# 64 bytes of padding behind the split-weight and transposed-x buffers of a two-layer decoder trunk

## The chip, the cores and the metric

The kernel runs on one core of one Trainium2 chip. The metric is the device time of the whole program in microseconds (us); lower is better. The kernel before was timed in three runs: 1771.68, 1772.74 and 1776.7 us, median 1772.74 us.

## The reference

The program computes a two-layer causal decoder trunk on x of 256 tokens by 2048 channels in float32. Cut to what matters for the time:

```
for layer in (0, 1):
    x = x + mixer(rmsnorm(x))          # layer 0: conv module and sparse attention, with w_in (2048 x 4656), w_out (2048 x 2048)
                                       # layer 1: pooling mixer, four 512 x 512 maps
    h = rmsnorm(x) @ w1                # w1: 2048 x 8192
    x = x + square(relu(h)) @ w2       # w2: 8192 x 2048
return rmsnorm(x)
```

## The kernel before, in words

Every large matrix product is done in three passes, to keep float32 precision with a one-pass matmul format: a weight w is split into a rounded part `hi` and a rest `lo`, an activation X likewise into Xh and Xl, and the product is hi*Xh + hi*Xl + lo*Xh. Each such triple is three matmuls on TensorE, each with a stationary operand of 128x128 that is loaded first (a row PEld in the profile) and a moving operand of 256 or 512 columns that streams through.

The weights are used in some 390 units of 128 partitions x 2048 floats (8192 bytes in a partition). The class `Weights` loads a unit into one of three `wraw` buffers by DMA from SyncE's queue, then splits it in two or four pieces: ScalarE writes `whi` (line 147) and VectorE subtracts to get `wlo` (recorded at line 78, where a small wrapper calls VectorE). `whi` and `wlo` have three buffers each, used in turn. Transposed x lies in four `xT` buffers of 8192 bytes, one for each group of 512 channels; each holds four k-tiles, with 256 columns of Xh and 256 of Xl in each.

The order of all instructions is written out by the program: no scheduler reorders it. Two kinds of matmul groups alternate.

- **256-column matmuls**: `unit_cols` (mixer) and `unit_wide` / `first_hidden` (MLP) load a 128x128 piece of `whi` or `wlo` as stationary operand and stream 256 columns of `xT`. One unit of weights meets the four `xT` buffers one after the other, 12 matmuls for each.
- **512-column matmuls**: `product` and its like load a 128x128 piece of the split hidden activations (buffers f11, f12, s1 to s4 and f22, shown in rows as `f` or `s`) and stream 512 columns of `whi` or `wlo`. `by_token` does the same in the output projection, with stationary pieces of `yo` (which lies in two `xT` buffers) or of `yc`.

An MLP layer runs over eight chunks of hidden channels. Inside the loop over seven of them each chunk does 8 tiles of 48 matmuls with 256 columns (the next chunk's hidden values) and 14 products of 12 matmuls with 512 columns (a Strassen-like scheme; VectorE adds weight units in `z` and `b` for it). So the two layers have 14 such chunks.

All matmuls are recorded at line 194 (a wrapper `mm`); transposes at line 232. So groups of rows are told apart by their tiles' names.

Of the kernel before, what the change touches and what calls it, by code (L numbers as in the profile page):

```python
# [27 lines left out]
F32 = mybir.dt.float32  # L28
F32R = mybir.dt.float32r
# [5 lines left out]
P = 128  # L35
S = 256
D = 2048
# [13 lines left out]
WARM = 2  # L51
RHO, SLACK, CATCH_UP = 0.99, 1.0, 1.1
W_BUFS = 3

CHUNKS = 8
MIX_UNITS = 52
# [26 lines left out]
class Weights:  # L83
# [13 lines left out]
    def load(self, pieces=1):  # L97
        u, n = self.loaded, D // pieces
        use = self.uses[u]
        self.loaded += 1  # L100
        if "z" in use:
            for tiles, name, bufs in ((self.z, "z", 2), (self.b, "b", 1)):
                t = tiles[use["set"]] = self.zpool.tile([P, D], F32, tag=name, bufs=bufs, name=name)
                self.nc.sync.dma_start(t, self.src[use[name]])
        if "raw" not in use:
            return
        t = self.pool.tile([P, D], F32, tag="raw", bufs=RAW_BUFS, name="wraw")
        self.raw[u] = t
        for i in range(pieces):
            self.nc.sync.dma_start(t[:, i * n:(i + 1) * n], self.src[use["raw"], :, i * n:(i + 1) * n])  # L110
            yield
# [22 lines left out]
    def pieces(self):  # L134

        nc = self.nc
        while self.split < self.n:
            if self.split >= PLAIN:
                use = self.uses[self.split]
                raw = self.raw.pop(self.split) if "raw" in use else {"z": self.z, "b": self.b}[use["from"]][use["set"]]  # L140
                hi = self.pool.tile([P, D], F32R, tag="whi", bufs=W_BUFS, name="whi")
                lo = self.pool.tile([P, D], F32R, tag="wlo", bufs=W_BUFS, name="wlo")
                self.parts[self.split] = (hi, lo)
                cut = self.cut
                for h in range(cut):
                    c = slice(h * (D // cut), (h + 1) * (D // cut))
                    nc.scalar.activation(hi[:, c], raw[:, c], AF.Copy)  # L147
                    self.done = (h + 0.5) / cut
                    yield
                    if self.queue:  # L150
                        self.queue.pop(0)()
                    self.vector.tensor_sub(lo[:, c], raw[:, c], hi[:, c].bitcast(F32))
                    self.done = (h + 1) / cut
                    if h < cut - 1:
                        yield
                self.then(use, raw)
            self.split += 1
            self.done = 0.0
            yield
# [20 lines left out]
def trunk(ctx: ExitStack, tc: tile.TileContext, a: dict, out: bass.AP, dump: dict | None = None):  # L180
# [5 lines left out]
    act = ctx.enter_context(tc.tile_pool(name="act", bufs=1, side="left"))  # L186
# [42 lines left out]
    def transpose(out, src):  # L229
        n = src.shape[0]  # L230
        pe[0] += 0.218
        nc.tensor.transpose(out, src, ident[0:n, 0:n])  # L232

    def split_evac(hi, lo, src):
        nc.scalar.activation(hi, src, AF.Copy)
        vector.tensor_sub(lo, src, hi.bitcast(F32))

    xT = [None] * 4

    x = None  # L240

    def turn_x(dc, g0, bank):

        xT[dc] = act.tile([P, 4, 512], F32R, tag="xT", bufs=4, name="xT")
        rest = []
        for h in range(2):
            t = bank().rearrange("p (f t) -> p f t", f=2)
            for f in range(2):
                d = (4 * dc + 2 * h + f) * P
                for tok in range(2):  # L250
                    transpose(t[:, f, tok * P:(tok + 1) * P], x[:, tok, d:d + P])
            for f in range(2):
                dt = 4 * dc + 2 * h + f
                o, g = xT[dc][:, 2 * h + f], vec[:, g0 + dt:g0 + dt + 1]
                nc.scalar.activation(o[:, 0:256], t[:, f], AF.Copy, scale=g)
                rest.append(lambda o=o, t=t[:, f], g=g: vector.scalar_tensor_tensor(
                    o[:, 256:512], t, g, o[:, 0:256].bitcast(F32), op0=ALU.mult, op1=ALU.subtract))
        for r in rest:
            r()
# [16 lines left out]
    with ExitStack() as mx:  # L276
        mix = mx.enter_context(tc.tile_pool(name="mix", bufs=1, side="right", reuse_waits="tile"))
# [44 lines left out]
        def start_steps():  # L322
            yield lambda: (token_sum(sq[0][:, 0], pss), vector.tensor_copy(r0, rms(pss, CONV / D)))
            yield lambda: (to_rows(r0, acc1(), rbc), split_x())

        def split_x():
            lo = []
            for j in range(4):
                xn = xraw[:, 4 * j:4 * j + 4]
                vector.tensor_tensor(xn, x32[j // 2][:, 4 * (j % 2):4 * (j % 2) + 4],  # L330
                                        rbc[:, None].to_broadcast([P, 4, 256]), op=ALU.mult)
                t = act.tile([P, 4, 512], F32R, tag="xT", bufs=4, name="xT")
                nc.scalar.activation(t[:, :, 0:256], xn, AF.Copy)
                lo.append(lambda t=t, xn=xn: vector.tensor_sub(t[:, :, 256:512], xn, t[:, :, 0:256].bitcast(F32)))
                if j:
                    lo.pop(0)()
                xT[j] = t
            lo.pop(0)()
            W.hold = False
# [108 lines left out]
        for i in range(2):  # L448
            t = mix.tile([P, KT, P], F32, tag="q8", bufs=2, name="w1")
# [5 lines left out]
        for i in range(2):  # L455
            t = mix.tile([P, 512], F32, tag="tt", bufs=3, name="wgl")[:, 0:384]
# [154 lines left out]
        def bank(tag, dt=F32):  # L611
            return ps.tile([P, 512], dt, tag=tag, bufs=2, name=tag)
# [40 lines left out]
        def transposed():  # L653
            for s in Tt:
                if callable(Tt[s]):
                    Tt[s] = Tt[s]()
# [194 lines left out]
        yo = []  # L851

        def o_transposed(m, b):
            if not yo:
                yo.extend(act.tile([P, 4, 512], F32R, tag="xT", bufs=4, name="yo") for _ in range(2))
            transposed()
            tp = bank("T")
            for d2 in range(2):
                dt = 4 * m + 2 * b + d2
                for tok in range(2):  # L860
                    transpose(tp[:, d2 * 256 + tok * P:d2 * 256 + (tok + 1) * P], o_tok[:, tok, dt * P:(dt + 1) * P])
            split_evac(yo[m][:, 2 * b:2 * b + 2, 0:256], yo[m][:, 2 * b:2 * b + 2, 256:512],
                       tp.rearrange("p (d t) -> p d t", d=2))
# [3 lines left out]
        for j in range(8):  # L867
            if j == 7:
                steps[2] = both(steps[2], one(o_transposed, 0, 0))
                steps[3] = both(steps[3], one(o_transposed, 0, 1))  # L870
# [35 lines left out]
        xt = [None] * 4  # L906

        def load_x(i, n, tag, bufs):
            t = (act if tag == "xT" else mix).tile([P, 2, n * 512], F32, tag=tag, bufs=bufs, name="xt",
                                                   padded_shape=[P, 2, 1024])  # L910
            nc.sync.dma_start(t, a["xn"][:, :, i * 512:(i + n) * 512])
            for q in range(n):
                xt[i + q] = t[:, :, q * 512:(q + 1) * 512]

        load_x(0, 2, "xT", 4)
        load_x(2, 1, "xT", 4)

        def o_half():
# [62 lines left out]
        for dc, u in O_ORDER:  # L981
            if u == 0:
                accs[dc] = [bank3() for _ in range(2)]

            def finish():
                for tok in range(2):
                    vector.tensor_add(x[:, tok, dc * 512:(dc + 1) * 512], xt[dc][:, tok], accs[dc][tok])
                turns.extend([lambda: None, lambda dc=dc: turn_x(dc, V_MLP0, bank3)])

            out_unit(accs[dc], yc[u], u, beside_conv, finish)  # L990
# [241 lines left out]
    def after0(dc):  # L1232
        add_squares(dc, ssq1)
        if dc == 0:
            pm_parts.extend(load_pm(i) for i in range(3))
            ps_row.extend(row(a["pool_scale"]))
        elif pm_parts:
            pm_parts.pop(0)()
        return [lambda: turn_x(dc, V_MIX1, bank3)]
# [33 lines left out]
    def pool_and_first():  # L1273


        units = first_hidden([lambda dc=dc: turn_x(dc, V_MLP1, bank3) for dc in (1, 2, 3)])
        next(units)
        pool_mean(2, z2)
        next(units)
        pool_mean(3, z3)  # L1280
        yield from units
# [146 lines left out]
```

## Time and profile before

| what | value |
|---|---|
| three runs | 1771.68, 1772.74, 1776.7 us (median 1772.74) |
| the profiled execution's own time | 1777.96 us |
| its span, first to last instruction | 1776.2 us |
| mean granted TensorE clock | 0.997 of full speed |
| TensorE busy | 1752.6 us of the span (99%), 11726 matmuls |
| VectorE busy | 1518.5 us (85%) |
| ScalarE busy | 1084.6 us (61%) |

The busy time of TensorE is the union of its matmuls. The matmuls overlap, so the mean time of one (277 to 284 ns for 256 columns) is more than the time from one start to the next; how long a matmul holds the engine is read from the starts of rows in the timeline.

### The profile page before, as it was taken

What the parts mean: (1) busy time and instruction counts of PE and PEld (TensorE: products, weight loads), DVE (VectorE), ACT (ScalarE), POOL (GpSimd) and SP (SyncE); (2) the same over time, 40 slices, a digit from 0 to 9 for tenths busy, and PEclk for the clock granted to TensorE, in tenths of its full rate; (3) what the DMA queues carried; (4) which work ended last, traced back from release to release, by engine and by line L of the source; (5) the groups of instructions that cost most, each with busy time, mean ns of one, the idle gap of its engine ahead of it and who ended that gap; (6) DMA issues with size and microseconds to landing.
All of it is one profiled execution on the core that took longest, in us unless ns stands there. A gap on an engine that the chain in (4) does not pass through costs nothing.

```text
span 1776.2 us, 28729 instructions
## 1 busy us (share of the span) xinstructions
PE 1752.6 (99%) x11726; PEld 1595.4 (90%) x11726; DVE 1518.5 (85%) x1888; ACT 1084.6 (61%) x1626; POOL 59.7 (3%) x80
## 2 busy tenths in 40 slices
PE   9999999999999999999999999999999999999997
PEld 7999998889898899999898989988989898989885
DVE  6998997766989898898989868798988989898984
ACT  4445666547666666666666655766666666666663
POOL 1000000000000000000000000000000000000000
PEclk9999999999999999999999999999999999999998
DMA  7654323546778787878777764687878787778772
GB/s 274 237 197 143 120 96 134 199 167 227 259 248 253 236 248 236 276 230 295 232 248 247 230 228 155 232 256 238 257 237 271 233 294 233 249 243 259 247 245 97
DMA packets 58052, 399.89 MB, mean 225 GB/s; under 512 B 6560, under 2 KB 6960, under 8 KB 10816
## 3 DMA queue, kind: packets, MB, share of 16 engines
q1 hardware_dynamic: 47760, 333.47, 48.9%
q0 software_dynamic: 8576, 61.43, 18.5%
q10 hardware_dynamic: 1584, 3.16, 0.5%
q8 instruction: 92, 1.51, 0.3%
q14 instruction: 40, 0.33, 0.0%
HBM read 395.93 MB, written 2.10 MB: 224 GB/s over the span
## 4 chain that ended last, share of the span: by engine, by line
PE 78%; DVE 18%; ACT 2%; issue 1%; DMA 1%; ACTq 0%; POOLq 0%; SPq 0%; DVEq 0%
PE acc L194 73%; DVE wlo L78 9%; DVE z L78 3%; DVE s L78 3%; PE S L194 2%; DVE x L78 2%; PE PV L194 1%; ACT whi L147 1%; PE T L232 1%; PE acc L232 1%; DVE f L78 0%; DMA xraw<-in_xT 0%; ACT t L1026 0%; DMA ident<-in_ident 0%; ACT t L1025 0%
## 5 line engine op out<-in xcount | busy, mean ns | idle before, releaser
L194 PE MATMUL acc<-xT,whi 128*128 128x256 f32 x4992 | 872.1, 279 | 0.0
L194 PEld LDWEIGHTS acc<-xT,whi 128*128 128x128 f32 x4992 | 764.8, 188 | 10.1
L78 DVE TENSOR_TENSOR wlo<-wraw,whi 128x1024 fp32r<-128x1024 f32 (+1 forms) x552 | 604.9, 1126 | 143.7 <-ACT whi L147 142.8
L194 PE MATMUL acc<-xT,wlo 128*128 128x256 f32 x2496 | 694.0, 278 | 0.0
L147 ACT ACTIVATE whi<-wraw 128x1024 fp32r<-128x1024 f32 (+1 forms) x552 | 515.2, 974 | 105.1 <-PE acc L194 86.5
L194 PEld LDWEIGHTS acc<-xT,wlo 128*128 128x128 f32 x2496 | 470.7, 189 | 0.0
L194 PE MATMUL acc<-whi,s 128*128 128x512 f32 x960 | 318.5, 393 | 2.8 <-DVE s L78 1.6
L78 DVE TENSOR_TENSOR wlo<-z,whi 128x1024 fp32r<-128x1024 f32 x224 | 267.1, 1219 | 47.9 <-ACT whi L147 47.1
L147 ACT ACTIVATE whi<-z 128x1024 fp32r<-128x1024 f32 x224 | 230.5, 1054 | 94.2 <-DVE z L78 73.3
L194 PE MATMUL acc<-whi,f 128*128 128x512 f32 x864 | 283.0, 392 | 0.0
L194 PEld LDWEIGHTS acc<-whi,s 128*128 128x128 f32 x960 | 179.3, 188 | 42.2 <-DVE s L78 7.5
L1025 ACT ACTIVATE t<-acc 128x256 f32<-128x256 f32 x128 | 48.8, 381 | 251.6 <-PE acc L194 250.8
L194 PE MATMUL acc<-wlo,s 128*128 128x512 f32 x480 | 190.8, 397 | 1.1
L194 PEld LDWEIGHTS acc<-whi,f 128*128 128x128 f32 x864 | 162.4, 188 | 32.2
L194 PE MATMUL acc<-wlo,f 128*128 128x512 f32 x432 | 169.4, 392 | 0.0
L78 DVE SCALAR_TENSOR_TENSOR x<-acc,r,x 128x512 f32<-128x512 f32 x156 | 116.4, 746 | 14.4 <-PE acc L194 14.2
L194 PEld LDWEIGHTS acc<-wlo,s 128*128 128x128 f32 x480 | 90.1, 188 | 28.2 <-DVE wlo L78 9.7
L78 DVE SCALAR_TENSOR_TENSOR ctile<-ctile,cw 128x256 f32<-128x256 f32 x240 | 101.5, 475 | 0.1
L194 PEld LDWEIGHTS acc<-wlo,f 128*128 128x128 f32 x432 | 81.1, 188 | 16.0
L1070 ACT ACTIVATE s<-s 128x512 fp32r<-128x512 f32 x56 | 35.4, 632 | 72.1 <-DVE s L78 72.1
L78 DVE TENSOR_TENSOR z<-z,wraw 128x1024 f32<-128x1024 f32 x56 | 65.9, 1219 | 0.0
L78 DVE TENSOR_TENSOR z<-z,b 128x1024 f32<-128x1024 f32 x56 | 65.9, 1219 | 0.0
(206 smaller groups left out, 1361.4 us busy)
## 6 DMA issues: line engine op xcount, KB each, us to landing
wraw<-in_ws SPq DMA_DIRECT2D x254, 1024.0 KB, 6.3
z<-in_ws SPq DMA_DIRECT2D x28, 1024.0 KB, 7.4
b<-in_ws SPq DMA_DIRECT2D x28, 1024.0 KB, 4.8
b<-in_ws POOLq DMA_DIRECT2D x28, 1024.0 KB, 8.8
z<-in_ws POOLq DMA_DIRECT2D x28, 1024.0 KB, 8.2
xraw<-in_xT SPq DMA_DIRECT2D x4, 512.0 KB, 7.5
wraw<-in_ws SPq DMA_DIRECT2D x8, 256.0 KB, 7.4
w<-in_cmp_w POOLq DMA_DIRECT2D x2, 1024.0 KB, 7.6
```

Of the source, the lines that this page charges most:

```text
L78: return fn(*args, **kw)
L147: nc.scalar.activation(hi[:, c], raw[:, c], AF.Copy)
L194: nc.tensor.matmul(out, w, x, **kw)
L232: nc.tensor.transpose(out, src, ident[0:n, 0:n])
L1025: nc.scalar.activation(out, acc, AF.Relu)
L1070: nc.scalar.activation(F[tag][:, :, 0:P], src(), AF.Copy)
```

## The change

Every `whi`, `wlo` and `xT` buffer (and `yo`, which shares xT's buffers) gets 16 floats, 64 bytes, behind its 8192. The tiles themselves are cut back to the same 2048 floats. One load of x in `load_x` no longer asks for a padded shape. The order of the instructions, their shapes and their waits are the same on all engines; only addresses differ.

```
+SKEW = 16
...
-                hi = self.pool.tile([P, D], F32R, tag="whi", bufs=W_BUFS, name="whi")
-                lo = self.pool.tile([P, D], F32R, tag="wlo", bufs=W_BUFS, name="wlo")
+                hi = self.pool.tile([P, D + SKEW], F32R, tag="whi", bufs=W_BUFS, name="whi")[:, 0:D]
+                lo = self.pool.tile([P, D + SKEW], F32R, tag="wlo", bufs=W_BUFS, name="wlo")[:, 0:D]
...
+    def skewed(name):
+        t = act.tile([P, D + SKEW], F32R, tag="xT", bufs=4, name=name)
+        return t[:, 0:D].rearrange("p (k t) -> p k t", k=4)
...
-        xT[dc] = act.tile([P, 4, 512], F32R, tag="xT", bufs=4, name="xT")
+        xT[dc] = skewed("xT")
...
-                t = act.tile([P, 4, 512], F32R, tag="xT", bufs=4, name="xT")
+                t = skewed("xT")
...
-                yo.extend(act.tile([P, 4, 512], F32R, tag="xT", bufs=4, name="yo") for _ in range(2))
+                yo.extend(skewed("yo") for _ in range(2))
...
-            t = (act if tag == "xT" else mix).tile([P, 2, n * 512], F32, tag=tag, bufs=bufs, name="xt",
-                                                   padded_shape=[P, 2, 1024])
+            t = (act if tag == "xT" else mix).tile([P, 2, n * 512], F32, tag=tag, bufs=bufs, name="xt")
```

Where the buffers start in each partition, in bytes, in the two built programs (in brackets the start modulo 512):

| buffers | before | after |
|---|---|---|
| whi, three | 48928, 57120, 65312 (all 288) | 48928, 57184, 65440 (288, 352, 416) |
| wlo, three | 73504, 81696, 89888 (all 288) | 73696, 81952, 90208 (480, 32, 96) |
| xT, four | 115424, 123616, 131808, 140000 (all 224) | 115808, 124064, 132320, 140576 (96, 160, 224, 288) |
| f11 to f22, seven | 193504 to 225248 (all 480) | the same |
| yc, two | 155232, 163424 (both 96) | the same |
| wraw, three | 24352, 32544, 40736 (all 288) | the same |
| z, two | 168928, 177120 (both 480) | the same |

Within a tile, the pieces that one matmul loads or streams start at multiples of 512 bytes. So the distance from the streaming piece to the piece that is loaded meanwhile, modulo 512, is the same for all matmuls of one pair of buffers. Here "distance" is the start of the stationary piece less the start of the moving piece, modulo 512:

| loaded while streaming | before | after (i = 0 to 2 the weight buffer, j = 0 to 3 the xT buffer) |
|---|---|---|
| whi while xT streams | 64 | 192 + 64(i - j): 0 to 320 |
| wlo while xT streams | 64 | 384 + 64(i - j): 192 to 448, and 0 |
| f or s while whi streams | 192 | 192, 128, 64 |
| f or s while wlo streams | 192 | 0, 448, 384 |
| yo while whi or wlo streams | 448 | varies |
| yc while whi streams | 320 | 320, 256, 192 |
| yc while wlo streams | 320 | 128, 64, 0 |

## Rows read from the trace of the kernel before

**Rows 1.** The page's head and its busy time of two engines.
```profile
span 1776.2 us, 28729 instructions
...
PE 1752.6 (99%) x11726; PEld 1595.4 (90%) x11726; DVE 1518.5 (85%) x1888; ACT 1084.6 (61%) x1626; POOL 59.7 (3%) x80
```

**Rows 2.** The page's chain that ended last, by engine and by line.
```profile
PE 78%; DVE 18%; ACT 2%; issue 1%; DMA 1%; ACTq 0%; POOLq 0%; SPq 0%; DVEq 0%
PE acc L194 73%; DVE wlo L78 9%; DVE z L78 3%; DVE s L78 3%; PE S L194 2%; DVE x L78 2%; PE PV L194 1%; ACT whi L147 1%; PE T L232 1%; PE acc L232 1%; DVE f L78 0%; DMA xraw<-in_xT 0%; ACT t L1026 0%; DMA ident<-in_ident 0%; ACT t L1025 0%
```

**Rows 3.** Costliest matmul groups, whole span: count | busy us, mean ns | idle before.
```profile
L194 PE MATMUL acc<-xT,whi 128*128 128x256 f32 x4992 | 872.1, 279 | 0.0
L194 PE MATMUL acc<-xT,wlo 128*128 128x256 f32 x2496 | 694.0, 278 | 0.0
L194 PE MATMUL acc<-whi,s 128*128 128x512 f32 x960 | 318.5, 393 | 2.8 <-DVE s L78 1.6
L194 PE MATMUL acc<-whi,f 128*128 128x512 f32 x864 | 283.0, 392 | 0.0
```

**Rows 4.** Timeline of PE, first and last row of one stretch: start, length.
```profile
748.27 0.28 PE L194 MATMUL acc<-xT,wlo 128*128 128x256 f32 x1
...
752.87 0.28 PE L194 MATMUL acc<-xT,wlo 128*128 128x256 f32 x1
```

**Rows 5.** The same for a later stretch, with its first row after 512-column matmuls.
```profile
798.07 0.40 PE L194 MATMUL acc<-xT,whi 128*128 128x256 f32 x2
...
799.00 0.28 PE L194 MATMUL acc<-xT,wlo 128*128 128x256 f32 x1
...
803.42 0.28 PE L194 MATMUL acc<-xT,wlo 128*128 128x256 f32 x1
```

**Rows 6.** The chain in order of time: start, length, what; five chunks' pieces.
```profile
534.05 58.60 PE acc L194 x394
618.51 58.60 PE acc L194 x394
702.98 58.60 PE acc L194 x394
787.45 57.36 PE acc L194 x394
870.67 57.36 PE acc L194 x394
```

**Rows 7.** One matmul group in the windows 37:270, 537:786 and 1125:1715 us.
```profile
L194 PE MATMUL acc<-xT,wlo 128*128 128x256 f32 x444 | 124.6, 281 | 0.0
...
L194 PE MATMUL acc<-xT,wlo 128*128 128x256 f32 x383 | 107.7, 281 | 0.0
...
L194 PE MATMUL acc<-xT,wlo 128*128 128x256 f32 x926 | 256.2, 277 | 0.0
```

**Rows 8.** Timeline, 512 columns with f loaded, in an MLP chunk.
```profile
806.51 0.39 PE L194 MATMUL acc<-wlo,f 128*128 128x512 f32 x1
...
808.57 0.39 PE L194 MATMUL acc<-wlo,f 128*128 128x512 f32 x1
```

**Rows 9.** Timeline, 512 columns with yo loaded, then with yc loaded, output projection.
```profile
324.87 0.39 PE L194 MATMUL S<-wlo,yo 128*128 128x512 f32 x1
...
329.67 0.39 PE L194 MATMUL S<-wlo,yo 128*128 128x512 f32 x1
...
365.60 0.39 PE L194 MATMUL acc<-wlo,yc 128*128 128x512 f32 x1
...
372.60 0.40 PE L194 MATMUL acc<-wlo,yc 128*128 128x512 f32 x1
```

**Rows 10.** VectorE's subtractions that write wlo, from two kinds of source buffers.
```profile
L78 DVE TENSOR_TENSOR wlo<-wraw,whi 128x1024 fp32r<-128x1024 f32 x456 | 541.7, 1219 | 128.6 <-ACT whi L147 127.9
L78 DVE TENSOR_TENSOR wlo<-z,whi 128x1024 fp32r<-128x1024 f32 x224 | 267.1, 1219 | 47.9 <-ACT whi L147 47.1
```

## The prediction

> **What bounds the kernel now.** I read the page first. TensorE is busy for 1752.6 of 1776.2 us, VectorE for 85% of the span [rows 1]. The chain that ended last lies on TensorE for 78% and on VectorE for 18%, and 73 points of TensorE's part are matmuls of line 194 [rows 2]. So the pace at which matmuls follow each other sets most of the time. Two kinds hold nearly all of it: 4992 + 2496 = 7488 matmuls of 256 columns on xT, and the 512-column products on f and s, 960 + 864 with whi and, as the code has one lo for two hi, 480 + 432 with wlo, 2736 in all [rows 3].
>
> Then the timeline, where the pace is read from starts. In the stretch from 748.27 to 752.87 us thirteen triples, 39 matmuls of 256 columns, take 4.60 us: 117.9 ns each [rows 4]. From 799.00 to 803.42 us the same 39 take 4.42 us: 113.3 ns each [rows 5]. The same instructions on the same kind of buffers thus have two rhythms, 4.6 ns or 4% apart. Each holds for hundreds of us: the group's mean length is 281 ns in the windows 37 to 270 and 537 to 786 us and 277 ns from 1125 to 1715 us [rows 7], so the length tells the rhythm of a whole window.
>
> The chain in order of time gives the price for a chunk. TensorE's piece of 394 matmuls takes 58.60 us in the three chunks from 534.05, 618.51 and 702.98 us and 57.36 us in those from 787.45 and 870.67 us [rows 6]: 1.24 us more in the slow rhythm. What lies between the end of one piece and the start of the next is 84.46 - 58.60 = 25.86 us in a slow chunk and 83.22 - 57.36 = 25.86 us in a fast one. That part belongs to VectorE, and TensorE's rhythm does not move it. So about 57.4 of 83.2, or 0.69, of what a slower or faster rhythm does to matmuls in a chunk reaches the end.
>
> **What is known of distance.** In the kernel before, every matmul on xT streams at distance 64 from the piece that is loaded meanwhile, and both rhythms occur there. So distance alone doesn't set the rhythm; it seems to be a state that the two streams fall into and keep. But distance does matter somewhere: in the output projection the loop, the weights and the shapes are the same for yo and yc, yet 21 matmuls with yo take 4.80 us, 228.6 ns each, and 30 with yc take 7.00 us, 233.3 ns each [rows 9]. Yo stands at distance 448, yc at 320. The f products, at distance 192, take 2.06 us for nine: 228.9 ns [rows 8]. So of three distances seen with 512 columns, one is 4.4 to 4.7 ns dearer.
>
> **The change part by part.** No instruction is added, removed or moved, and no wait. VectorE's and ScalarE's work on the shifted buffers I put at nothing: the subtraction takes 1219 ns with wraw as source, which starts at 288 modulo 512 as whi does, and 1219 ns with z, which starts at 480 [rows 10]. Distance doesn't show there; were it to show, VectorE's 18% of the chain [rows 2] would be the part that pays. Transfers keep their sizes and their order. The cost or gain is therefore in the rhythm of matmuls alone.
>
> (a) 256 columns. After the change the distance is one of eight multiples of 64, differs between hi and lo within a triple, and changes each time that the weights meet the next xT buffer, every 12 matmuls. Below, the bound is the fast rhythm everywhere, 113.3 ns; above, the slow one everywhere, 117.9 ns. The trace shows neither mixed distances nor most of the eight. What it does show is the price of settling: after a 512-column group the first eight intervals of the fast stretch take 799.00 - 798.07 = 0.93 us where eight steady ones take 0.907 [rows 5], so 24 ns are lost before the fast rhythm is found. If each of the 7488 / 12 = 624 groups paid that, it would be 15 us, and times 0.69 10 us. I take the middle of the two rhythms, 115.6 ns, as a pair of streams that is disturbed every 12 matmuls should sit in neither; twelve fast matmuls with one settling come to 115.3, close to it.
>
> The sum for (a): in three slow chunks half of 1.24 is saved, in the eleven others half is lost: 8 x 0.62 = +5.0 us. In the mixer, 28 units of 48 = 1344 matmuls now slow (281 ns in the window 37 to 270 [rows 7]) gain 2.3 ns each: -3.1 us. The two first hidden chunks, 768 matmuls, now fast, lose 2.3 ns: +1.8 us. Together +3.7 us.
>
> (b) 512 columns. F and s go from the constant distance 192 to a mix of 192, 128, 64 with hi and 0, 448, 384 with lo. I take the middle of the two seen paces, 228.9 and 233.3: +2.2 ns. Inside the loop there are 14 chunks of 168: 2352 x 2.2 x 0.69 = +3.6 us; the last products of each layer are 384 more: +0.8 us. Yc, now at the dear distance, gets back 192 x 2.2 = 0.4 us, and yo loses as much. Together +4.4 us. Bounds: nothing, or 233.3 everywhere, +8.8 us. A gain below 228.9 has no row.
>
> The sum is +3.7 + 4.4 = +8.1 us against the profiled execution's 1777.96 (span 1776.2 and 1.8 around it): 1786. The median of the runs is 5.2 us lower than that execution, perhaps because fewer of their chunks fell into the slow rhythm. Set on the median, 1772.74 + 8.1 is **1781 us**.
>
> **The rule that speaks against the change.** The yc rows cost 4.4 to 4.7 ns more than the yo rows [rows 9], which says that TensorE's load and its stream can hinder each other. The Trainium skill, "SBUF — State Buffer", section "Who interferes with whom", gives TensorE two independent read ports, one for the moving operand and one for weight loads, and says that TensorE never waits on anyone. By that the change would do nothing and the time stay at 1773; the yc rows don't bear it out, the two rhythms at one distance might.
>
> **Rivals.**
> - *No effect.* The rhythm is set by when the streams start, not by where the buffers lie. For it: both rhythms at distance 64 [rows 4, 5], and a rhythm that survives hundreds of changes between 512 and 256 columns [rows 7]. Against it: yc [rows 9]. Time 1773, 0.3% either way for what share happens to be slow. Chance 0.22.
> - *Faster: the slow rhythm goes.* If equal distance is what lets the two streams stay in step in the bad way, varying it breaks the slow rhythm and leaves the fast one: -3 x 1.24 in chunks and -1344 x 4.6 ns = -6.2 in the mixer, -9.9 us with (b) at nothing: 1763. For it: the slow rhythm lasts so long undisturbed. Against it: the same holds of the fast one, which is the more common and would be disturbed as well. It decides if fewer than a third of the groups keep to 117.9. Chance 0.27.
> - *Slow everywhere.* The streams never find the fast rhythm within 12 matmuls: +11 x 1.24 = 13.6, first chunks 768 x 4.6 ns = +3.5, (b) at 233.3 +8.8: +26 us, 1799. For it: the mixer, where work is most mixed, is slow in its whole window [rows 7]. Chance 0.19.
>
> **How the numbers follow.** My forecast, between the rhythms, has 0.32 and is the likeliest: 1781, its own range 1776 to 1788. About 0.3% (5.3 us) is what a measurement of this kernel can tell from no change. Slower: all of 0.19 and most of 0.32, 0.47. Same: 0.22 and the forecast's low end, 0.25. Faster: 0.28. The range for 8 in 10 runs from the fast rhythm everywhere, 1763, to nearly the slow one everywhere, 1798.
>
> **What would show it.** In the profile after, the mean length of the 256-column groups should stand near 279 ns in all windows, not 277 or 281, and starts within 12 matmuls should be uneven, with the excess at the head. TensorE's piece of 394 matmuls should lie near 58 us in every chunk, not at two values. F and s products should come at about 231 ns. VectorE's 1219 ns should stay. I am wrong if the two rhythms remain as they are (no effect), if all chunks come to 57.4 us or less (faster), or if a distance not seen so far, 0 or 128 or 256, has a pace outside 113.3 to 117.9 ns: that is what no row here bounds.

## The result: 1.43% slower

The changed kernel takes 1799.33 us (median of four runs, 1799.15 to 1801.42), the kernel before on the same chip 1774.72 us (four runs, 1771.68 to 1777.52): a ratio of 1.0143, 95% interval 1.0129 to 1.0157. The forecast had the sign, but 1781 us and a range that ended at 1798. The time is that of the rival "slow everywhere", 1799.

The page of the changed kernel, its head and its busy time (line numbers are two higher than before up to the MLP):

```profile
span 1799.6 us, 28729 instructions
...
PE 1779.2 (99%) x11726; PEld 1621.4 (90%) x11726; DVE 1520.4 (84%) x1888; ACT 1085.5 (60%) x1626; POOL 59.7 (3%) x80
```

Against [rows 1] TensorE's busy time grows by 26.6 us and VectorE's by 1.9. The instructions are the same in number. So all of it is pace. The costliest matmul groups, to be held against [rows 3]:

```profile
L196 PE MATMUL acc<-xT,whi 128*128 128x256 f32 x4992 | 893.4, 282 | 0.0
L196 PE MATMUL acc<-xT,wlo 128*128 128x256 f32 x2496 | 699.4, 280 | 0.0
L196 PE MATMUL acc<-whi,s 128*128 128x512 f32 x960 | 320.3, 395 | 2.0 <-DVE s L80 0.7
L196 PE MATMUL acc<-whi,f 128*128 128x512 f32 x864 | 284.8, 394 | 0.0
```

Two rows of the timeline, eleven triples apart within one stretch of 256-column matmuls, answer to [rows 4] and [rows 5]:

```profile
826.86 0.28 PE L196 MATMUL acc<-xT,wlo 128*128 128x256 f32 x1
...
830.77 0.28 PE L196 MATMUL acc<-xT,wlo 128*128 128x256 f32 x1
```

Eleven triples, 33 matmuls, in 3.91 us: 118.5 ns each, where the two rhythms of before had 117.9 and 113.3. The same group in the windows 37 to 270, 537 to 786 and 1125 to 1715 us answers to [rows 7]:

```profile
L196 PE MATMUL acc<-xT,wlo 128*128 128x256 f32 x444 | 124.2, 280 | 0.0
...
L196 PE MATMUL acc<-xT,wlo 128*128 128x256 f32 x373 | 104.6, 280 | 0.0
...
L196 PE MATMUL acc<-xT,wlo 128*128 128x256 f32 x920 | 257.9, 280 | 0.0
```

Before, these were 281, 281 and 277: no window has the fast rhythm any more. The length alone would mislead here: 280 is less than the slow rhythm's 281, but from start to start the matmuls of these windows come at 117.7, 118.0 and 118.0 ns, where the kernel before has 117.2, 117.8 and 113.8. The chain in order of time answers to [rows 6]:

```profile
539.20 58.80 PE acc L196 x394
623.87 58.91 PE acc L196 x394
708.64 58.80 PE acc L196 x394
793.30 58.81 PE acc L196 x394
877.98 58.92 PE acc L196 x394
```

A chunk's piece of TensorE takes 58.80 to 58.92 us, 1.4 to 1.6 more than before in a fast chunk. What is left of a chunk is 623.87 - 539.20 - 58.80 = 25.87 us, as before to 0.01. And VectorE's subtractions, against [rows 10]:

```profile
L80 DVE TENSOR_TENSOR wlo<-wraw,whi 128x1024 fp32r<-128x1024 f32 x456 | 542.6, 1221 | 141.5 <-ACT whi L149 139.7
L80 DVE TENSOR_TENSOR wlo<-z,whi 128x1024 fp32r<-128x1024 f32 x224 | 267.1, 1219 | 53.7 <-ACT whi L149 53.7
```

A second measure is used below. The mean "pace" of a kernel is the mean time from one start to the next in its trace: for 256 columns over some 7300 pairs of successive matmuls on xT with a load of whi or wlo between them (pairs further apart than 130 ns left out), for 512 columns over some 2570 pairs on f and s (over 250 ns left out). Kernel before: 115.0 and 229.2 ns. Changed kernel: 117.9 and 231.7 ns.

### The profile page after: what moved, and what is told of

Its sections match the earlier page's. It is cut to its first block, busy times and chain, and to the rows that moved or that the text cites. A ratio compares the mean times of both kernels' runs of the same rounds, so it can differ in the third digit from the quotient of the medians.

```text
span 1799.6 us, 28729 instructions
## 1 busy us (share of the span) xinstructions
PE 1779.2 (99%) x11726; PEld 1621.4 (90%) x11726; DVE 1520.4 (84%) x1888; ACT 1085.5 (60%) x1626; POOL 59.7 (3%) x80
## 4 chain that ended last, share of the span: by engine, by line
PE 78%; DVE 18%; ACT 2%; issue 1%; DMA 0%; ACTq 0%; POOLq 0%; DVEq 0%
PE acc L196 74%; DVE wlo L80 9%; DVE z L80 3%; DVE s L80 3%; DVE x L80 2%; PE S L196 2%; PE PV L196 1%; ACT whi L149 1%; PE T L234 1%; PE acc L234 1%; DVE f L80 0%; ACT t L1031 0%; ACT t L1030 0%; DMA vec<-in_vec 0%; PE T L196 0%
## 5 line engine op out<-in xcount | busy, mean ns | idle before, releaser
L196 PE MATMUL acc<-xT,whi 128*128 128x256 f32 x4992 | 893.4, 282 | 0.0
L80 DVE TENSOR_TENSOR wlo<-z,whi 128x1024 fp32r<-128x1024 f32 x224 | 267.1, 1219 | 53.7 <-ACT whi L149 53.7
L80 DVE TENSOR_TENSOR z<-z,b 128x1024 f32<-128x1024 f32 x56 | 65.9, 1219 | 0.0
L80 DVE TENSOR_TENSOR z<-z,wraw 128x1024 f32<-128x1024 f32 x56 | 65.9, 1219 | 0.0
```

The source lines that it names most:

```text
L80: return fn(*args, **kw)
L196: nc.tensor.matmul(out, w, x, **kw)
```

## The experiments

Three theories stood at the start of the experiments. A: the fast rhythm needs a distance that stays the same for long, and variation destroys it. B: the value of the distance decides, and the change moved most matmuls to dear values. C: hi and lo at unequal distance within a triple do the harm. Where paces are given by distance, the addresses of the built program were laid beside the matmuls of the trace, in order. All kernels compute the whole reference. The pads are tiles that nothing uses; they only move what comes after them. `xr` is the buffer ahead of xT.

**Parts of the change.** e1 takes the skew from whi and wlo, e2 from xT:

```
e1: hi = self.pool.tile([P, D], ...); lo = self.pool.tile([P, D], ...)     # xT keeps D + SKEW
e2: t = act.tile([P, D], F32R, tag="xT", bufs=4, name=name)                # whi, wlo keep D + SKEW
```

> Only the xT buffers (and yo) get the 64 bytes; whi and wlo stay 8192 bytes apart. The distance of weights to streaming xT is 64, 0, 448 or 384 by xT buffer, the same for hi and lo, and changes every 12 matmuls; f and s stay at 192. Theory A (the fast rhythm needs a distance that stays the same over many groups): 256-column matmuls at some 118 ns as in the changed kernel, f and s at 229 ns, about 1793 us. Theory B (it is the particular distance that counts, 64 is fast and others are slow): one xT buffer in four fast, about 1789 us. Theory C (hi and lo at unequal distance within a triple break the rhythm): as before, about 1775 us.

Measured: 1794.99 us, ratio 1.0094 (1.0074 to 1.0114), paces 117.7 and 229.6 ns. By xT buffer the pace is 115.2 ns at distance 64, 118.8 at 0, 117.9 at 448 and 118.9 at 384: the buffer at 64 alone is quick. So C is not needed for the harm, as hi and lo are at equal distance here; the value of the distance seems to count, as B has it, but A is not yet out.

> Only whi and wlo get the 64 bytes; the four xT buffers stay 8192 bytes apart. Distance of whi to streaming xT is 192, 256 or 320 and of wlo 384, 448 or 0 by weight buffer, so it changes every 48 matmuls and differs between hi and lo; f and s vary as in the changed kernel. Theory A: 256-column matmuls mostly slow, 117 to 118 ns, but with time to settle within 48, 1790 to 1799 us. Theory B: slow, about 1799 us. Theory C: slow, about 1799 us. If the xT side alone did the harm: f and s at 231 ns alone, about 1780 us.

Measured: 1794.70 us, ratio 1.0092 (1.0068 to 1.0116), paces 117.3 and 231.3 ns. Either half of the change does most of the harm alone, so the two don't add. Each of the three weight buffers has another pair of distances here, and they have paces of their own. One tile of 48 matmuls with hi at 320 and lo at 0, and the next with hi at 192 and lo at 384:

```profile
539.67 0.29 PE L196 MATMUL acc<-xT,wlo 128*128 128x256 f32 x1
...
544.97 0.28 PE L196 MATMUL acc<-xT,wlo 128*128 128x256 f32 x1
...
548.08 0.28 PE L196 MATMUL acc<-xT,wlo 128*128 128x256 f32 x1
...
553.28 0.27 PE L196 MATMUL acc<-xT,wlo 128*128 128x256 f32 x1
```

Both spans are 15 triples, 45 matmuls: 5.30 us or 117.8 ns each, and 5.20 us or 115.6 ns each.

**Constant distances.** e3 sets hi and lo apart; e4 to e9, e11 and e12 move the xT buffers alone by one pad, so that one distance holds for all 7488 matmuls:

```
e3:        hi = ...
      +    if self.split == PLAIN:                           # once, ahead of the first lo
      +        self.pool.tile([P, 48], F32, name="pad")
           lo = ...
e4 to e9, e11, e12, behind the line that makes xraw:
+    act.tile([P, n], F32, name="pad")    # n = 96, 16, 64, 80, 128, 48, 8, 56 in that order
```

> No skew; one unused 192-byte pad between the whi and the wlo buffers, so that every distance is constant but hi and lo differ: whi 384 and wlo 64 to streaming xT, f and s 192 to whi and 0 to wlo. Theory A: fast rhythm for 256 columns, some 113 to 115 ns, the rest from f and s at distance 0 (up to +8 us), 1775 to 1783 us. Theory B: two of three loads at a distance not seen fast, 116 to 118 ns, 1785 to 1799 us. Theory C: all slow, 118 ns, 1793 to 1799 us.

Measured: 1808.35 us, ratio 1.0169 (1.0148 to 1.0189), paces 119.0 and 233.4 ns. The slowest of all, with every distance constant. The chain in order of time of this run shows one piece that covers seven chunks:

```profile
454.15 590.13 PE acc L196 x3790
```

TensorE is now so slow that VectorE's share of a chunk no longer ends last anywhere in it.

> No skew; one unused 384-byte pad ahead of xT, so that all weights stand at the constant distance 192 to streaming xT, hi and lo alike (before: 64); f and s stay at 192. Theory A: 113 to 115 ns for 256 columns, about 1775 us. Theory B: if 192 is a slow distance, 118 ns and about 1793 us; if it is a fast one, 1770 to 1775 us. Theory C: about 1775 us.

Measured: 1794.46 us (four runs within 0.21 us), ratio 1.0091 (1.0071 to 1.0111), pace 117.7 ns. Nothing varies, and the fast rhythm is gone. So a distance that stays the same is not enough for it, and A does not explain this run; whether variation does harm by itself is left to e13 and e14. In e4 yo stood at 320 in place of 448 and came at 233.3 ns in place of 229.4, as yc did at 320 in the kernel before.

> No skew; an unused 64-byte pad ahead of xT, so that all weights stand at the constant distance 0 to streaming xT; f and s at 192, yo at 0. If the value of the distance sets the rhythm: in the run at 192 the 31 loads of the gate weights stood at 0 and came at 113.4 ns, so 113 to 114 ns and 1766 to 1770 us. If 64 was lucky and any other constant is slow as 192 was: 117.8 ns and 1794 us.

> No skew; an unused 320-byte pad ahead of xT: constant distance 256 to streaming xT, f and s at 192, yo at 256. If the distance counts modulo 256: the same as at 0, within 2 us. If modulo 512: no row shows it; anything from 113.3 to 119 ns, 1766 to 1800 us. If 64 was lucky: 1794 us.

Measured: 1806.61 us at 0, ratio 1.0168 (1.0151 to 1.0186), and 1806.35 us at 256, ratio 1.0167 (1.0150 to 1.0184); pace 119.9 ns in both. My expectation for 0, drawn from 31 loads of the gate weights, was wrong. Those load pieces of 64 or 112 columns, not of 128, and have another order of distances: 113.4 ns at 0 (e4) and 118.3 at 320 (e5). The costliest groups of e5 and then of e7:

```profile
L194 PE MATMUL acc<-xT,whi 128*128 128x256 f32 x4992 | 907.5, 284 | 0.0
L194 PE MATMUL acc<-xT,wlo 128*128 128x256 f32 x2496 | 706.3, 283 | 0.0
```

```profile
L194 PE MATMUL acc<-xT,whi 128*128 128x256 f32 x4992 | 907.5, 284 | 0.0
L194 PE MATMUL acc<-xT,wlo 128*128 128x256 f32 x2496 | 706.3, 283 | 0.0
```

Two kernels with xT 256 bytes apart agree to the last digit in these groups, and both take 1.7% longer than the kernel before, whose xT lies 64 bytes from that of e5. The chain in order of time of e5:

```profile
541.68 59.12 PE acc L194 x394
626.67 59.12 PE acc L194 x394
```

The rest of the chunk is 626.67 - 541.68 - 59.12 = 25.87 us here too.

> No skew; an unused 256-byte pad ahead of xT: constant distance 320 to streaming xT, f and s at 192, yo at 192. If the distance counts modulo 256: like the kernel before at 64, two rhythms, 1772 to 1781 us. If modulo 512: in the run at 192, 181 loads of xT stood at 320 to 256 streaming columns of weights and came at 114.2 ns, so fast, 1766 to 1772 us. If 64 was lucky: 1794 us.

> No skew; an unused 512-byte pad ahead of xT, so every distance modulo 512 is what it was before, 64 and 192, but xT lies at another absolute place. If the distance counts modulo 512 or a divisor: like the kernel before, two rhythms, 1772 to 1781 us. If a longer period or the absolute place counts: another rhythm, up to 1795 us.

Measured: 1778.93 us at 320, ratio 1.0009 (0.9997 to 1.0020), and 1777.38 us at 64 with xT 512 bytes further on, ratio 1.0005 (0.9992 to 1.0017); paces 115.4 and 115.2 ns. Both have two rhythms, as the kernel before has; in e6's chain in order of time:

```profile
1242.70 58.60 PE acc L194 x394
1327.17 57.38 PE acc L194 x394
```

So 64 and 320 are one class, and 0 and 256 another: the distance counts modulo 256. In the kernel before and in e6 and e8 each of the 112 tiles of 48 matmuls in the MLP's loops keeps, behind its first 12, to 113.3 or to 117.7 or 117.8 ns; 88, 72 and 80 of them have the fast rhythm.

> No skew; an unused 192-byte pad ahead of xT: constant distance 384, that is 128 modulo 256, to streaming xT; f and s at 192, yo at 128. It completes the four classes of 64 bytes. If the class alone sets the rhythm: in two earlier runs the 31 loads of gate weights stood at 128 and came at 117.7 ns, so 117.7 ns and about 1794 us, as at 192. If mixing in the changed kernel costs extra, the mean of the four classes stays well under its 118.0 ns; if not, this run should come near 119 ns, 1800 us.

Measured: 1807.46 us, ratio 1.0169 (1.0146 to 1.0192), pace 119.6 ns; dearer than the 31 loads of gate weights (117.7 ns) had suggested.

> No skew; an unused 32-byte pad ahead of xT: constant distance 32, and xT starts at a multiple of 64 while the weights keep 32 past one. If only the class of 64 bytes counts, with both starts rounded down, it should be like 0 or like 64: 1806 or 1777 us. If half steps have rhythms of their own: anything from 1765 to 1810 us; a value under 1770 would mean that the fast rhythm alone is left.

> No skew; an unused 224-byte pad ahead of xT: constant distance 352, 96 modulo 256, with xT at a multiple of 64. Rounded to classes of 64: like 64 or like 128, 1777 or 1794 us. If half steps have rhythms of their own: anything from 1765 to 1810 us; under 1770 means the fast rhythm alone.

Measured: 1797.93 us at 32, ratio 1.0117 (1.0094 to 1.0140), and 1800.03 us at 96, ratio 1.0129 (1.0101 to 1.0156); paces 118.3 and 118.5 ns. Half steps have paces of their own, and neither has the fast rhythm.

**The 512-column side.** e10 and e16 move all weight buffers, x and xT together, so that xT stays at 64 and f and s change class; e15 moves weights and xT as e10 does, and f and s as well, so that these are at 192 modulo 256 again:

```
e10, e15: +    const.tile([P, 48], F32, name="pad")     # ahead of wpool; 16 floats in e16
e15:      +    mlp.tile([P, 16], F32, name="pad2")      # last tile of the MLP pool: moves f and s by 64 the other way
```

> No skew; an unused 192-byte pad ahead of all weight buffers: xT's distance stays 64 as before, f and s go from 192 to 0, yc from 320 to 128. For 512 columns yo and xT at 0 came at 227.4 to 228.0 ns where f at 192 comes at 228.9 to 229.8. If that holds for f and s: 1.5 ns less on 2736 matmuls, of which some 0.69 counts, 1772 to 1775 us beside 1777 for before; if the 256-column rhythm falls fast or slow by another accident, 1768 to 1782 us. If f at 0 is as dear as in the mixed kernel (234 to 237 ns): 1790 us.

Measured: 1782.08 us, ratio 1.0035 (1.0021 to 1.0049), paces 116.5 and 227.1 ns. Two groups of this run:

```profile
L195 PE MATMUL acc<-whi,s 128*128 128x512 f32 x960 | 316.5, 391 | 2.3 <-DVE s L78 1.1
L195 PE MATMUL acc<-whi,f 128*128 128x512 f32 x864 | 280.9, 389 | 0.0
```

The 512-column matmuls are 2.1 ns quicker, but the 256-column ones of the MLP now keep mostly to the slow rhythm (117.4 ns between 1120 us and the end), which costs more.

> No skew; weight buffers, x and xT moved by 64 bytes: xT at 64 as before, f and s at 128, yc at 0. In the mixed kernel f at 128 came at 232 ns: 2.5 ns more on 2736 matmuls, some +5 us. If the 512-column class decides which rhythm the 256 columns take up after it: all fast, -8 us, sum 1774, or all slow, +16 us, sum 1798. If it does not: 1782 us.

Measured: 1782.77 us, ratio 1.0045 (1.0030 to 1.0060), paces 114.7 and 232.1 ns. Here the 256-column rhythm is mostly fast. The 512 columns are 2.9 ns dearer, 7.9 us of TensorE's time on 2736 matmuls; with the chunks' share of 0.69 some 6 of these reach the end, most of the 7 us. One row of its chain in order of time:

```profile
530.97 57.99 PE acc L195 x394
```

> No skew; all weight buffers, x and xT moved by 192 bytes as in the run with f at 0, where the mixer's 256-column matmuls came at 114.7 ns and not 117.3, and the split hidden buffers moved by 64 the other way, so that f and s are at 192 modulo 256 again. If the mixer keeps that rhythm and the MLP falls as before: 3 to 4 us less than before, 1773. If the rhythm is an accident of each run: as before, 1777 us.

Measured: 1774.86 us, ratio 0.9999 (0.9989 to 1.0008). The mixer came at 116.8 ns (37 to 270 us), where e10 had 114.1, and the MLP mostly at the fast rhythm: the opposite of what was aimed at. Which of the two rhythms a stretch takes is not steered by this, and no version here beats the kernel before.

**Variation alone.** e13 keeps the skew but makes it 256 bytes, on whi; e14 skews xT by 128 bytes:

```
e13:  hi = self.pool.tile([P, D + 64], F32R, tag="whi", bufs=W_BUFS, name="whi")[:, 0:D]
e14:  SKEW = 32, on xT alone
```

> The skew is kept but made 256 bytes, and put on the three whi buffers alone (all that fits): the distance of whi to streaming xT is 64 or 320 by buffer and that of wlo 64, f and s at 192 or 448, so distances vary modulo 512 and not modulo 256. If variation itself does the harm: like the changed kernel's weights alone, 1790 to 1799 us. If only the class modulo 256 counts: like the kernel before, two rhythms, 1772 to 1782 us.

Measured: 1773.40 us, ratio 0.9995 (0.9986 to 1.0004), pace 114.3 ns. The distances vary between 64 and 320, one class, and nothing is lost. Its chain in order of time has both rhythms, as before:

```profile
447.45 58.57 PE acc L194 x394
...
698.36 57.37 PE acc L194 x394
```

> Only xT is skewed, by 128 bytes: distances of weights to the four xT buffers 64, 192, 64 and 192 modulo 256, hi and lo alike, f and s at 192. If the classes simply add: half at each, (1777 + 1794) / 2 = 1786 us. If change within a unit costs extra or keeps the fast rhythm away: all at 117.8 ns, 1794 us or more.

Measured: 1783.94 us, ratio 1.0051 (1.0037 to 1.0065), pace 116.1 ns. By distance: 115.1 ns at 64 and 113.9 at 320, 117.6 at 192 and 117.8 at 448. Groups of 12 matmuls at a good class find the fast pace at once between groups at a dear one. Its chunks, in order of time:

```profile
785.83 58.03 PE acc L196 x394
869.73 58.03 PE acc L196 x394
```

58.03 lies between 57.37 and 58.60: half of the groups at each pace.

The constant distances side by side (paces in ns, times in us; the 512-column pace at 64 is that of yc in [rows 9]; the pace at 64 is that of the kernel before, e6, e8, e10, e15 and e16, the time that of e8):

| distance modulo 256 | 256 columns on xT | time | 512 columns on whi and wlo |
|---|---|---|---|
| 0 | 119.9 (e5, e7) | 1807, 1806 | 227.1 (e10) |
| 64 | 114.6 to 116.5, two rhythms | 1777 | 233.3 |
| 128 | 119.6 (e9) | 1807 | 232.1 (e16) |
| 192 | 117.7 (e4) | 1794 | 229.2 (before) |

**Unequal hi and lo.** In the changed kernel hi and lo of a triple never stand in the same class; four pairs occur, equally often. The table has the 256-column pace of each, in ns, taken from the start of a triple to the start of the next with the same buffers. The mean of classes takes the paces of the table above, with 115.2 at 64, and counts hi twice.

| hi and lo, modulo 256 | mean of classes | one pair for 48 matmuls or more | changed kernel, 12 at a time |
|---|---|---|---|
| 192 and 128 | 118.3 | 116.2 (e2) | 118.3 |
| 0 and 192 | 119.2 | 117.8 (e2) | 117.9 |
| 64 and 0 | 116.8 | 117.8 (e2) | 117.8 |
| 128 and 64 | 118.1 | 118.9 (e3) | 118.6 |

Classes don't add here. The pair 192 and 128 in e2 is quicker than either class alone, and the pairs with 64 in them have no fast rhythm. In the changed kernel all four lie within 0.8 ns. With hi and lo alike, and 12 matmuls at a time, the classes do show: 115.2 to 118.9 ns in e1, 113.9 to 117.8 in e14.

## Why the prediction was wrong

**What bounds the kernel**: right. The pace of matmuls is all that moved. VectorE's 1219 ns stayed, with 1221 for one group. The 25.86 us of a chunk that TensorE's pace doesn't touch stayed at 25.87 in the changed kernel and in e5; e3 shows where that ends, when TensorE is slow enough to cover it.

**Term (b), 512 columns**: right in size, with luck. I forecast +2.2 ns, and the pace went from 229.2 to 231.7, +2.5. But it is not a middle of two seen paces. By triples, the changed kernel has 233.7 ns with hi at 192 and lo at 0, dearer than either class alone (229.2 and 227.1; e3, with this pair throughout, came at 233.4), 231.8 with hi at 128 and lo at 192, and 229.8 with hi at 64 and lo at 128, cheaper than either (233.3 and 232.1). So with unequal hi and lo 512 columns don't follow the classes either, and go both ways.

**Term (a), 256 columns**: this step failed. It read "I take the middle of the two rhythms, 115.6 ns, as a pair of streams that is disturbed every 12 matmuls should sit in neither". Measured: 117.9 ns. Behind it stood the reading that distance alone doesn't set the rhythm, since both rhythms occur at 64. That is only half true. Class 64 allows two rhythms; the classes 0, 128 and 192 have no fast one, with constant distance over the whole kernel (e4, e5, e7, e9), and 0 and 128, at 119.9 and 119.6, lie above the bound of 117.9 that I had taken from the slow rhythm. The change gives three of four triples a hi in those classes. The fourth has hi at 64, but lo at 0, and comes at 117.8 too. So no part of the changed kernel has a fast rhythm that could pull its pace down to the middle.

The mean of the four classes, (119.9 + 115 + 119.6 + 117.7) / 4, is 118.0, and the changed kernel has 117.9. That agreement is no proof that classes add: the same mean, hi counted twice, gives 118.0 for e2, which came at 117.3, and 118.1 for e3, which came at 119.0, and by pairs the changed kernel does not follow it. Change of distance by itself does no harm where hi and lo are alike in class (e13, e14). For unequal pairs that is not so clear: 192 and 128 take 116.2 ns for 48 matmuls at a time in e2 and 118.3 for 12 at a time in the changed kernel. The settling of 24 ns per group that I priced shows behind 512 columns (in layer 1 of the kernel before the first 12 matmuls of a tile come at 115.3 ns, the others at 113.3), but not from one xT buffer to the next: in e14 a group of 12 at distance 320 has 113.9 ns on the mean.

In us: 117.9 - 115.6 = 2.3 ns more than forecast on 7488 matmuls are 17 us of TensorE's time, and some three quarters of that reach the end, 13 us. Together with the kernel before's own median, which rose from 1772.74 to 1774.72 with the fourth run, that is 15 of the 18 us by which the forecast fell short. The sign that I had named for my forecast, a mean length near 279 ns in all windows, nearly came (280) and proved nothing, as the starts show.

**That distance matters at all**: right, and the yc rows [rows 9] had said so: yc's class is 64, the dearest for 512 columns. In e4 yo came to the same class and to the same 233.3 ns. Where I went wrong was to bound 256 columns by the two rhythms at one distance and not to ask what the other distances cost there: the classes span 114 to 120 ns, and in another order. The prediction did say that no row bounded 0, 128 or 256.

**Distance and not place**: e9 and e15 have their xT buffers at the same addresses (the first at 115616) and the weights 192 bytes apart, and come at 119.6 and 114.6 ns. So it is the distance that counts, not where xT lies. Nor is it wraw, into which DMA writes meanwhile: in e2 xT and wraw lie alike for all tiles, and the pace goes by the weight buffer. Whether the loads from whi and wlo do it or the writes of ScalarE and VectorE into them is parted by no run of its own. That all 112 tiles of e4 in the loops come at 117.7 or 117.8 ns, though ScalarE is busy for only some 60% of the time, speaks for the loads.

**The rivals.** "No effect" is refuted by the result and by e4, e5 and e9: moving xT by 64 bytes (e5) takes the pace from 115.0 to 119.9 ns with nothing else changed. The Trainium skill ("SBUF — State Buffer", section "Who interferes with whom") says that TensorE's two read ports are independent and that it never waits; for these loads the runs do not bear that out, and the measurement decides. "Faster" had the slow rhythm go; what went is the fast one. "Slow everywhere" named the time, 1799, but not the reason: I had put it down to streams that don't find the fast rhythm within 12 matmuls, which the groups of 12 at distance 320 in e14 do (113.9 ns), and to 512 columns at 233.3 ns, which came at 231.7. That it hit the time is luck.

**What stays open.** What decides between the two rhythms at 64 was not found. The kernel before ran between 1771.3 and 1781.8 us on these chips, while the four runs of e4 stayed within 0.21 us. In its trace the rhythm flips twice among the tiles of the MLP's loops, from 524 to 536 and from 778 to 790 us, both times between two chunks; in e16 it flips 55 times. That the load and the stream meet in parts of the memory that repeat every 256 bytes is the plainest reading of the table, but only the period is shown, not the mechanism. Why unequal hi and lo have the paces that they have, and why all pairs come near 118 ns in the changed kernel, is not known: no run holds each of the four pairs alone. A version with the fast rhythm alone was not found.

## What to carry to other kernels

When TensorE is the bound, look at the time from start to start of equal matmuls, not at its busy time or the mean length alone: two values a few per cent apart on the same shapes can point to where operands lie, as with yo and yc, though the two rhythms at 64 had the same addresses. Before skewing buffers at random, hold one distance constant over the whole kernel and step it; here the kernel before and three runs with one pad (e4, e5, e9) gave the column for 256 columns, and the best class was the one the kernel already had. A skew that keeps the good class (256 bytes here) is harmless. One that spreads hi and lo alike over the classes gives about the mean of them (e1, e14); one that sets hi and lo apart has to be measured.

## What the runs showed of the hardware

With one-pass float32 matmuls back to back, the distance between the stationary piece that is loaded and the moving piece that streams counts modulo 256 bytes: held constant, 256 columns take from 113.3 to 119.9 ns and 512 columns from 227.1 to 233.3 ns, by class, at the same granted clock of 0.996 to 0.998. The order of the classes is not the same for the two widths: 0 is the best for 512 columns and the worst for 256. At distance 64 the 256-column stream has two stable rhythms, 113.3 and 117.9 ns, at the same addresses. Where hi and lo of a triple stand in different classes, the pace is not the mean of theirs: 116.2 ns for 256 columns at 192 and 128 (117.7 and 119.6 alone), 233.7 ns for 512 columns at 192 and 0 (229.2 and 227.1 alone).
